# Feature-major outputs by stationary weight columns in a two-block float32 transformer kernel

## The chip, the cores and the metric

The kernel runs on one core of a Trainium2 chip. The metric is the device time of one execution in microseconds. A core has TensorE (matmuls, "PE" in the profile, and its weight loads, "PEld"), VectorE ("DVE"), ScalarE ("ACT"), GpSimd ("POOL") and SyncE ("SP", which issues most DMAs). A matmul multiplies a stationary operand (loaded first, 128 rows by up to 128 columns) with a moving one (128 rows by up to 512 columns) and adds into a bank of PSUM.

## The reference

For 256 tokens of width 2048, float32 throughout, the reference computes two transformer blocks in sequence:

```
x = x + concat(ssd(conv4(xbc)), fox_attention(q, k, v)) @ w_out      # z, xbc, dt, q, k, v, f = rmsnorm(x) @ w_in
x = x + peer(rmsnorm(x), wq, k1, k2, u, v)                           # expert search: q = t @ wq, scores q.k1, q.k2, top 16
x = rmsnorm(x)
h = x + concat(moba_attention(q, k, v), conformer_conv(u)) @ w_out2  # q, k, v, u = rmsnorm(x) @ w_in2, conv of 31 taps
h = h + cross_attention(rmsnorm(h), rmsnorm(mem), wq_c, wk_c, wv_c, wo_c)
h = h + square(relu(rmsnorm(h) @ w1)) @ w2
out = rmsnorm(h)
```

A convolution here runs along the tokens, one filter per channel. Attention scores contract over the features of q and k. So the convolutions, the attention scores and the expert scores all want the features of their input on partitions and the tokens along the free dimension.

## The kernel before

Every activation that feeds a GEMM lies in SBUF feature-major (features on partitions, 256 tokens along the free dimension) as two tiles: a rounded part (`xh`, type fp32r) and the remainder (`xl`). Weights stream from HBM as `raw` tiles of 512 rows x 512 columns. `split_w` cuts each into two halves of 256 rows; of each half ACT makes the rounded part `whi` (line 117) and DVE the remainder `wlo` (line 118). Both have three buffers. A product is the sum of three: high x high, high x low, low x high.

`gemm_block` (line 150 issues its matmuls) makes one block of 512 output columns from 2048 rows of weights: for each of 16 row groups and each of 2 halves of the tokens it loads 128 tokens of the activation as the stationary operand and moves 512 weight columns past them, three times. This is 96 matmuls of 512 columns. The result is token-major: tokens on partitions, 512 features along the free dimension. `gemm_cols` (lines 178 and 182) does it the other way for `peer_u` and `w1`: 128 weight columns are stationary, and the tokens move, 512 columns (high and low side by side) for the high weights, 256 for the low. Its result is feature-major.

Blocks whose result is wanted feature-major, but come from `gemm_block`, go through three steps. First ACT reads the accumulators and multiplies each token's row by its 1 / rms (`r`, one number per partition), into `pre`, `uv`, `scr` or `c_..`. Then TensorE transposes 128 x 128 pieces (`tpose`, line 226). Then ACT copies the result (`tposed`, line 604), or the convolution reads it from PSUM. The second convolution's evacuation (lines 1150 and 1151) applies the sigmoid gate before its transposes.

`by_token` (lines 197 to 205) turns `r` into rows, the same 256 numbers on every partition: DVE multiplies the identity by `r` into `dg`, one matmul with a matrix of ones adds the columns up, ACT copies the result to `rtok`. It is used by `up` and by the last feed-forward layer.

All work beside the GEMMs is written as generators. `later` puts one in a lane, and `step(rate)`, called four times a block, takes as many pieces from the lanes as the rates say; `flush` does the same, ahead of them, for what follows a block's evacuation. The framework then orders each engine's instructions by its own estimate of when they are ready; `pin` keeps one in place. Each engine runs its queue in order. PSUM holds two buffers each of the two accumulators, of `tp` (transposes) and of `mm` (small products).

Of the kernel before, what the change touches and what calls it, by code (L numbers as in the profile page):

```python
# [9 lines left out]
F32 = mybir.dt.float32  # L10
# [9 lines left out]
P = 128  # L20
# [35 lines left out]
def build(tc, A, out):  # L56
# [4 lines left out]
    with es:  # L61
# [127 lines left out]

        def sums(o, acc):  # L190
# [5 lines left out]
        def by_token(r, pool):  # L196

            dg = pool.tile([P, 2, P], F32, name="dg", bufs=1)
# [4 lines left out]
            o = pool.tile([P, T], F32, name="rtok", bufs=1)  # L203
            nc.scalar.copy(o, pr[:, :T])
            return o.unsqueeze(1).to_broadcast([P, 2, T])
# [84 lines left out]
def front(env):  # L290
# [5 lines left out]
    with phase_pool(tc, "ssd", True) as sp:  # L296
# [37 lines left out]
        z.gemm_block(xh, xl, range(16), src0, pre0.append, raw0=raw0)  # L334
# [6 lines left out]
        r8 = main.tile([P, 2], F32, name="rstd1q")  # L341
        nc.vector.tensor_scalar_mul(r8, r, 0.125)
# [94 lines left out]
        def conv(nb, sb):  # L437
            for c2 in range(0, 4, 2):
                tp = z.tpose(lambda j, t: sb[:, t, (c2 + j) * P : (c2 + j + 1) * P])
                for j in range(2):  # L440
                    ch = nb * 4 + c2 + j
                    w = V["conv_w"][:, ch * 4 : ch * 4 + 4]
                    o = cv[:, ch]
                    nc.vector.tensor_scalar(
                        o, tp[:, j], w[:, 3:4], V["conv_b"][:, ch : ch + 1], OP.mult, OP.add
                    )
                    for tap in range(3):
                        sh = 3 - tap
                        nc.vector.scalar_tensor_tensor(
                            o[:, sh:], tp[:, j, : T - sh], w[:, tap : tap + 1], o[:, sh:], OP.mult, OP.add  # L450
                        )
                    yield
                c = nb * 4 + c2
                nc.scalar.activation(cv[:, c : c + 2], cv[:, c : c + 2], AF.Silu)
# [13 lines left out]
        z.gemm_block(xh, xl, range(16), src(2), evac_xbc(2))  # L468
# [132 lines left out]
        def tposed(o, sb):  # L601
            for c2 in range(0, 4, 2):
                tp = z.tpose(lambda j, t: sb[:, t, (c2 + j) * P : (c2 + j + 1) * P])
                nc.scalar.copy(o[:, c2 : c2 + 2], tp)
                yield

        env["tposed"] = tposed

        def qkv(half, pool):
            sb = {}  # L610

            def evac(n):
                def f(acc):
                    if n == "v":
                        sb[n] = pool.tile([P, 2, 512], F32, name="v_f")
                    else:
                        sb[n] = fp.tile([P, 2, 512], F32, name="pre", bufs=2)
                    rr = r8 if n == "q" else r
                    pre = sb[n]
                    for t in range(2):  # L620
                        nc.scalar.activation(pre[:, t], acc[t], AF.Copy, scale=rr[:, t : t + 1])
                    yield
                    if n != "v":
                        sb[n] = pool.tile([P, 4, T], F32, name=n + "T")
                        yield from tposed(sb[n], pre)

                return f

            for i, n in enumerate("qkv"):
                z.gemm_block(xh, xl, range(16), src(5 + 3 * half + i), evac(n))  # L630
            return half, sb["q"], sb["k"], sb["v"]
# [122 lines left out]
def peer(env):  # L754
# [7 lines left out]
    with phase_pool(tc, "peer") as pp:  # L762
# [10 lines left out]
        def scores(nb):  # L773


            def f(acc):
                k12 = k12s[:, nb % 2]
                nc.sync.dma_start(k12, A["k12"][:, nb * 4 : nb * 4 + 4])
                sb = scr[:, 0].rearrange("p (t c) -> p t c", t=2)
                for t in range(2):  # L780
                    nc.scalar.activation(sb[:, t], acc[t], AF.Copy, scale=r2[:, t : t + 1])
                yield
                qT = scr[:, 1].rearrange("p (c t) -> p c t", c=4)
                yield from env["tposed"](qT, sb)
# [235 lines left out]

        for nb in range(4):
# [55 lines left out]
def second(env):  # L1077
# [6 lines left out]
    tposed = env["tposed"]  # L1084
    with phase_pool(tc, "mix2") as fp:
# [4 lines left out]

        ap = ExitStack()
# [21 lines left out]
        def norm_conv():  # L1113
# [30 lines left out]
        for c in range(0, 8, 2):  # L1144

            def ev(acc, c=c):
                uv = fp.tile([P, 2, 512], F32, name="uv", bufs=2)
                for t in range(2):
# [11 lines left out]
            z.gemm_block(nh, nl, range(16), src(c // 2), ev, RATES["conv"])  # L1160


        def qkv(half):
            sb = {}

            def evac(n):
                def f(acc):
                    if n == "v":
                        pre = sb[n] = att.tile([P, 2, 512], F32, name="v_m", bufs=2)
                    else:  # L1170
                        pre = fp.tile([P, 2, 512], F32, name="uv", bufs=2)
                    for t in range(2):
                        nc.scalar.activation(pre[:, t], acc[t], AF.Copy, scale=r[:, t : t + 1])
                    yield
                    if n != "v":
                        sb[n] = att.tile([P, 4, T], F32, name=n + "T", bufs=2)
                        yield from tposed(sb[n], pre)

                return f

            for h in range(half * 4, half * 4 + 4):
                nc.sync.dma_start(bias[:, h], toeplitz(z.bd[h]))
            for i, n in enumerate("qkv"):
                z.gemm_block(nh, nl, range(16), src(4 + 3 * half + i), evac(n), RATES["qkv%d" % half])
            return half, sb["q"], sb["k"], sb["v"]
# [50 lines left out]
        def ev(n, rs):  # L1236
            def f(acc):
                sb = fp.tile([P, 2, 512], F32, name="c_" + n, tag="uv", bufs=2)
                for t in range(2):
# [277 lines left out]
```

## Time and profile before

| | |
|---|---|
| median of 3 runs | 3170.79 us (3170.75 to 3173.59) |
| the profiled execution | 3171.58 us, its span 3169.8 us |
| granted TensorE clock, mean | 0.999 |
| TensorE matmuls busy | 3150.7 us (99%), 15732 matmuls |
| weight loads busy | 2604.8 us (82%), 15733 loads |
| DVE busy | 2080.7 us (66%) |
| ACT busy | 1603.6 us (51%) |

The span runs from the first to the last instruction; the rest of the execution's time lies around it. Busy time is the union of an engine's instructions. Matmuls overlap each other in it, so that TensorE's busy share says that it is never without work, not how fast it goes.

### The profile page before, as it was taken

What the parts mean: (1) busy time and instruction counts of PE and PEld (TensorE: products, weight loads), DVE (VectorE), ACT (ScalarE), POOL (GpSimd) and SP (SyncE); (2) the same over time, 40 slices, a digit from 0 to 9 for tenths busy, and PEclk for the clock granted to TensorE, in tenths of its full rate; (3) what the DMA queues carried; (4) which work ended last, traced back from release to release, by engine and by line L of the source; (5) the groups of instructions that cost most, each with busy time, mean ns of one, the idle gap of its engine ahead of it and who ended that gap; (6) DMA issues with size and microseconds to landing.
All of it is one profiled execution on the core that took longest, in us unless ns stands there. A gap on an engine that the chain in (4) does not pass through costs nothing.

```text
span 3169.8 us, 39966 instructions
## 1 busy us (share of the span) xinstructions
PE 3150.7 (99%) x15732; PEld 2604.8 (82%) x15733; DVE 2080.7 (66%) x3013; ACT 1603.6 (51%) x2191; POOL 91.2 (3%) x123
## 2 busy tenths in 40 slices
PE   8999999999999999999999999999999999999998
PEld 7877788888888888888788887888788888888887
DVE  5765667899777756565555555898666655555565
ACT  5556555665555545444444445445756534444454
POOL 0000000000000001001000000000000000000000
PEclk9999999999999999999999999999999999999999
DMA  6444454565677777677767665555444555555554
GB/s 251 173 146 165 144 188 175 207 213 206 233 242 246 246 255 264 235 239 265 265 227 238 233 217 180 194 186 184 161 174 172 186 186 189 191 191 186 187 190 155
DMA packets 101645, 648.52 MB, mean 205 GB/s; under 512 B 11229, under 2 KB 12389, under 8 KB 32592
## 3 DMA queue, kind: packets, MB, share of 16 engines
q1 hardware_dynamic: 82512, 575.63, 51.6%
q0 software_dynamic: 18944, 70.33, 6.7%
q8 instruction: 123, 2.02, 0.3%
q14 instruction: 66, 0.54, 0.0%
HBM read 608.68 MB, written 37.24 MB: 204 GB/s over the span
## 4 chain that ended last, share of the span: by engine, by line
PE 98%; DMA 1%; ACT 0%; DVE 0%; SPq 0%; issue 0%; ACTq 0%
PE acc L150 59%; PE acc L178 23%; PE acc L182 11%; PE tp L226 1%; PE mm L903 1%; PE mm L749 0%; DMA raw<-in_w_in_dram 0%; PE mm L641 0%; PE tp L740 0%; PE mm L788 0%; ACT whi L117 0%; PE mm L563 0%; PE mm L638 0%; PE mm L750 0%; DVE wlo L118 0%; DMA raw<-in_peer_v_dram 0%
## 5 line engine op out<-in xcount | busy, mean ns | idle before, releaser
L118 DVE TENSOR_TENSOR wlo<-raw,whi 128x1024 fp32r<-128x1024 f32 x1065 | 1301.2, 1223 | 937.4 <-ACT whi L117 935.2
L117 ACT CAST whi<-raw 128x1024 fp32r<-128x1024 f32 x1065 | 1115.4, 1048 | 1287.2 <-PE acc L150 886.2
L150 PE MATMUL acc<-whi,hT 128*128 128x512 f32 x5300 | 1700.4, 398 | 8.2 <-ACT whi L117 8.2
L150 PEld LDWEIGHTS acc<-whi,hT 128*128 128x128 f32 x5300 | 993.3, 188 | 249.1 <-ACT whi L117 8.7
L178 PE MATMUL acc<-hT,whi 128*128 128x512 f32 x3072 | 1086.1, 397 | 0.0
L150 PE MATMUL acc<-wlo,hT 128*128 128x512 f32 x2650 | 1048.6, 396 | 1.7 <-DVE wlo L118 1.6
L182 PE MATMUL acc<-hT,wlo 128*128 128x256 f32 x3072 | 863.4, 281 | 0.0
L178 PEld LDWEIGHTS acc<-hT,whi 128*128 128x128 f32 x3072 | 576.7, 188 | 136.2
L150 PEld LDWEIGHTS acc<-wlo,hT 128*128 128x128 f32 x2650 | 497.6, 188 | 120.1 <-DVE wlo L118 3.7
L182 PEld LDWEIGHTS acc<-hT,wlo 128*128 128x128 f32 x3072 | 578.9, 188 | 0.3 <-DVE wlo L118 0.2
L1107 DVE SCALAR_TENSOR_TENSOR cc<-hc,vec,cc 128x256 f32<-128x256 f32 x240 | 102.1, 478 | 0.5
L193 ACT COPY at<-acc 128x256 f32<-128x256 f32 x128 | 48.0, 375 | 81.9 <-PE acc L182 81.9
L194 DVE TENSOR_TENSOR at<-acc,at 128x256 f32<-128x256 f32 x128 | 53.5, 419 | 20.0 <-ACT at L193 19.5
L193 ACT COPY hid<-acc 128x256 f32<-128x256 f32 x64 | 23.9, 373 | 48.3 <-PE acc L182 48.3
L681 DVE TENSOR_TENSOR x<-acc,x 128x512 f32<-128x512 f32 x72 | 46.4, 681 | 0.7 <-PE acc L150 0.6
L923 DVE TENSOR_TENSOR at<-at,rtok 128x512 f32<-128x512 f32 x64 | 43.9, 686 | 1.1
L194 DVE TENSOR_TENSOR hid<-acc,hid 128x256 f32<-128x256 f32 x64 | 26.9, 421 | 21.0 <-ACT hid L193 21.0
L971 DVE TENSOR_TENSOR hT<-ag,hT 128x1024 fp32r<-128x1024 f32 x32 | 38.9, 1217 | 0.0
L967 DVE TENSOR_TENSOR ag<-ag 128x1024 f32<-128x1024 f32 x32 | 38.9, 1216 | 0.0
L927 POOL DMA_DIRECT2D act<-at x32 | 17.5, 547 | 730.7 <-ACT at L925 686.2
L952 POOL DMA_DIRECT2D ag<-gd x32 | 37.4, 1168 | 3.9 <-DMA gd<-gs 2.5
L903 PE MATMUL mm<-ohA,ohB 128*128 128x128 f16 x512 | 35.9, 220 | 0.0
(314 smaller groups left out, 1499.2 us busy)
## 6 DMA issues: line engine op xcount, KB each, us to landing
raw<-in_peer_u_dram SPq DMA_DIRECT2D x128, 1024.0 KB, 5.0
raw<-in_peer_v_dram SPq DMA_DIRECT2D x128, 1024.0 KB, 4.9
raw<-in_w_dram SPq DMA_DIRECT2D x128, 1024.0 KB, 4.9
raw<-in_w_in_dram SPq DMA_DIRECT2D x83, 1024.0 KB, 4.9
raw<-in_w_out_dram SPq DMA_DIRECT2D x32, 1024.0 KB, 4.8
raw<-in_wq_dram SPq DMA_DIRECT2D x16, 1024.0 KB, 4.9
act<-at POOLq DMA_DIRECT2D x32, 512.0 KB, 7.1
gd<-gs POOLq DMA_DIRECT2D x16, 1024.0 KB, 6.2
```

The costliest lines, as they stand in the source:

```text
L117: nc.scalar.copy(hi[:, :kt, :n], raw[:, k0 : k0 + kt, :n])
L118: nc.vector.tensor_sub(lo[:, :kt, :n], raw[:, k0 : k0 + kt, :n], hi[:, :kt, :n].bitcast(F32))
L150: mm(o, a, b, start=start, stop=stop)
L178: mm(acc[c], hi[:, k, cs], x2[:, kk].rearrange("p a t -> p (a t)"), start=kk == 0, stop=False,)
L182: mm(acc[c][:, :T], lo[:, k, cs], x2[:, kk, 0], start=False, stop=kk == 15)
L193: nc.scalar.copy(o[:, c], acc[c][:, T:])
L194: nc.vector.tensor_add(o[:, c], acc[c][:, :T], o[:, c])
L681: nc.vector.tensor_add(x[:, t, sl], acc[t], x[:, t, sl])
L903: mm(pg[:, j], B2[:, tq + j], Ag[k][:, tq + j], start=k == 0, stop=k == 1)
L923: nc.vector.tensor_mul(at[:, 2 * b : 2 * b + 2], at[:, 2 * b : 2 * b + 2], rt)
L967: z.pin(nc.vector.tensor_mul(av, av, g.rearrange("p b c t -> p c b t")))
L1107: nc.vector.scalar_tensor_tensor(o, hc[:, c, tap : tap + T], w[:, tap : tap + 1], o, OP.mult, OP.add)
```

## The change

A new function `gemm_feat` makes a block of 512 output columns with 128 weight columns stationary and 256 tokens moving: for each of 16 row groups and 4 groups of columns, three matmuls of 256 columns. Two column groups share an accumulator bank. It takes the place of `gemm_block` for the inputs of both convolutions, for q and k of the three attentions, and for the expert search's queries; v stays with `gemm_block`. `scaled` evacuates it on DVE: it multiplies each accumulator by the rows of 1 / rms (and by 0.125 for the first attention's q). The transposes, their copies and `tposed` go. `by_token` is called for the scale vectors of the first and the second convolution, of the memory and of the cross attention as well; that of the expert search moves ahead of its GEMMs. The gate of the second convolution becomes a sigmoid over the feature-major half and one multiply. The squares of the second convolution's layer norm are made one channel group at a time.

```
+        def gemm_feat(xh, xl, src, evac, rate=2, raw0=None):
+            acc = [ps.tile([P, 512], F32, name="acc%d" % c) for c in range(2)]
+            for g in range(4):
+                raw = raw0 if raw0 is not None and g == 0 else load_w(src(g))
+                for k0 in range(0, 4, 2):
+                    hi, lo = split_w(raw, k0)
+                    for k in range(2):
+                        kk = 4 * g + k0 + k
+                        for c in range(4):
+                            cs = slice(c * P, c * P + P)
+                            o = acc[c // 2][:, c % 2 * T : c % 2 * T + T]
+                            mm(o, hi[:, k, cs], xh[:, kk], start=kk == 0 and c % 2 == 0, stop=False)
+                            mm(o, hi[:, k, cs], xl[:, kk], start=False, stop=False)
+                            mm(o, lo[:, k, cs], xh[:, kk], start=False, stop=kk == 15 and c % 2 == 1)
+                    flush()
+                step(rate)
+            after = evac([a.rearrange("p (c t) -> p c t", c=2) for a in acc])
...
+        def scaled(o, acc, rows, by=None):
+            for c in range(2):
+                oc = o[:, 2 * c : 2 * c + 2]
+                if by is None:
+                    nc.vector.tensor_mul(oc, acc[c], rows)
+                else:
+                    nc.vector.scalar_tensor_tensor(oc, acc[c], by, rows, OP.mult, OP.mult)
...
-        z.gemm_block(xh, xl, range(16), src(1), pre0.append)
+        z.gemm_feat(xh, xl, src(1), pre0.append)
         z.drain()
         r = z.rstd_of(ss, D, "rstd1")
...
+        rt = z.by_token(r, fp)
...
         def conv(nb, sb):
-            for c2 in range(0, 4, 2):
-                tp = z.tpose(lambda j, t: sb[:, t, (c2 + j) * P : (c2 + j + 1) * P])
...
         def evac_xbc(nb):
             def f(acc):
-                sb = fp.tile([P, 2, 512], F32, name="pre", bufs=2)
-                for t in range(2):
-                    nc.scalar.activation(sb[:, t], acc[t], AF.Copy, scale=r[:, t : t + 1])
+                sb = fp.tile([P, 4, T], F32, name="pre", bufs=2)
+                z.scaled(sb, acc, rt)
                 z.later(conv(nb, sb))
...
+        z.later(rows_of_rstd())
         for nb in range(4):
-            z.gemm_block(th, tl, range(16), lambda g: A["wq"][nb, g], scores(nb), RATES["wq"])
-        rt = z.by_token(r2, pp)
-        z.pin(nc.tensor.ldweights(iota))
+            z.gemm_feat(th, tl, lambda g: A["wq"][nb, g], scores(nb), RATES["wq"])
+        rt = rts[0]
...
-                sq = fp.tile([P, 2, T], F32, name="sq", bufs=1)
-                nc.scalar.activation(sq, cc[:, c : c + 2], AF.Square)
                 for j in range(2):
-                    mm(pv[:, :T], C["ones"], sq[:, j], start=c + j == 0, stop=c + j == 7)
+                    sq = fp.tile([P, T], F32, name="sq", bufs=1)
+                    nc.scalar.activation(sq, cc[:, c + j], AF.Square)
+                    mm(pv[:, :T], C["ones"], sq, start=c + j == 0, stop=c + j == 7)
...
             def ev(acc, c=c):
-                uv = fp.tile([P, 2, 512], F32, name="uv", bufs=2)
-                for t in range(2):
-                    a, g = uv[:, t, :T], uv[:, t, T:]
-                    nc.scalar.activation(g, acc[t][:, T:], AF.Sigmoid, scale=r[:, t : t + 1])
-                    nc.vector.scalar_tensor_tensor(a, acc[t][:, :T], r[:, t : t + 1], g, OP.mult, OP.mult)
-                yield
-                tp = z.tpose(lambda j, t: uv[:, t, j * P : j * P + P])
-                nc.scalar.copy(hc[:, c : c + 2, 30:], tp)
+                uv = fp.tile([P, 4, T], F32, name="uv", bufs=2)
+                z.scaled(uv, acc, rows[0])
+                nc.scalar.activation(uv[:, 2:], uv[:, 2:], AF.Sigmoid)
+                yield
+                nc.vector.tensor_mul(hc[:, c : c + 2, 30:], uv[:, :2], uv[:, 2:])
                 z.later(conv(c))
...
-            z.gemm_block(nh, nl, range(16), src(c // 2), ev, RATES["conv"])
+            z.gemm_feat(nh, nl, src(c // 2), ev, RATES["conv"])
```

Where instructions stand now, at three places. First TensorE, at the second attention's q block. Before, the matmuls of the block after it are under way (each row is one matmul of the token-major form), and the four transposes of a part of q stand between them:

```order
L150 MATMUL acc_17237<-whi,hT 128x512
L150 MATMUL acc_17238<-whi,hT 128x512
L150 MATMUL acc_17238<-wlo,hT 128x512
L150 MATMUL acc_17238<-whi,hT 128x512
L226 MATMUL tp<-con,uv 128x128 x4
L150 MATMUL acc_17237<-whi,hT 128x512
L150 MATMUL acc_17237<-wlo,hT 128x512
L150 MATMUL acc_17237<-whi,hT 128x512
```

After, the same place on TensorE, where the q block (`acc_18359`) ends and the k block (`acc_18632`, `acc_18633`) begins; lines 202 to 204 are the three products of `gemm_feat`:

```order
L202 MATMUL acc_18359<-hT,whi 128x256
L203 MATMUL acc_18359<-hT,whi 128x256
L204 MATMUL acc_18359<-hT,wlo 128x256
L202 MATMUL acc_18632<-hT,whi 128x256
L203 MATMUL acc_18632<-hT,whi 128x256
L204 MATMUL acc_18632<-hT,wlo 128x256
L202 MATMUL acc_18632<-hT,whi 128x256
L203 MATMUL acc_18632<-hT,whi 128x256
L204 MATMUL acc_18632<-hT,wlo 128x256
L202 MATMUL acc_18633<-hT,whi 128x256
```

No transposes stand in the k block, and each matmul has half as many columns.

Second, DVE at the start of the second block (`mix2`), where the final scale `rstd` of the first is made, x is scaled by it in two halves (128x2048), and the first convolution block is evacuated. Before:

```order
L1065 TENSOR_TENSOR rstd_16349<-rstd_16349,rstd_16341 128x2
L1069 TENSOR_SCALAR x<-x,rstd_16341 128x2048
L118 TENSOR_TENSOR wlo<-raw,whi 128x1024 x5
L1151 SCALAR_TENSOR_TENSOR uv<-acc_16364,rstd_16349,uv 128x256
L1151 SCALAR_TENSOR_TENSOR uv<-acc_16365,rstd_16349,uv 128x256
```

After, at the same place:

```order
L1082 TENSOR_TENSOR rstd_17279<-rstd_17279,rstd_17271 128x2
L1086 TENSOR_SCALAR x<-x,rstd_17271 128x2048
L231 TENSOR_SCALAR dg<-con,rstd_17279 128x128 x2
L118 TENSOR_TENSOR wlo<-raw,whi 128x1024 x5
L217 TENSOR_TENSOR uv<-acc_17294,rtok 128x512
L217 TENSOR_TENSOR uv<-acc_17295,rtok 128x512
L118 TENSOR_TENSOR wlo<-raw,whi 128x1024
L1174 TENSOR_TENSOR hc<-uv 128x2x256
```

Two multiplies for `dg` come in ahead of the next `wlo`, the evacuation is twice as wide, and the gate's multiply follows it. On TensorE the `by_token` matmul stands behind 102 matmuls of the first convolution block and 8 transposes of x.

Third, DVE in the second convolution, around the evacuation of its second block; the `cc` rows are the taps. Before:

```order
L118 TENSOR_TENSOR wlo<-raw,whi 128x1024
L1107 SCALAR_TENSOR_TENSOR cc<-hc,vec,cc 128x256
L1151 SCALAR_TENSOR_TENSOR uv<-acc_16527,rstd_16349,uv 128x256
L1107 SCALAR_TENSOR_TENSOR cc<-hc,vec,cc 128x256
L1151 SCALAR_TENSOR_TENSOR uv<-acc_16528,rstd_16349,uv 128x256
L1107 SCALAR_TENSOR_TENSOR cc<-hc,vec,cc 128x256
L118 TENSOR_TENSOR wlo<-raw,whi 128x1024
```

After:

```order
L118 TENSOR_TENSOR wlo<-raw,whi 128x1024
L1130 SCALAR_TENSOR_TENSOR cc<-hc,vec,cc 128x256
L217 TENSOR_TENSOR uv<-acc_17559,rtok 128x512
L1130 SCALAR_TENSOR_TENSOR cc<-hc,vec,cc 128x256
L217 TENSOR_TENSOR uv<-acc_17560,rtok 128x512
L1130 SCALAR_TENSOR_TENSOR cc<-hc,vec,cc 128x256
L118 TENSOR_TENSOR wlo<-raw,whi 128x1024
L1130 SCALAR_TENSOR_TENSOR cc<-hc,vec,cc 128x256
L1174 TENSOR_TENSOR hc<-uv 128x2x256
```

The evacuation's two operations are wider, and a third follows. From the first tap to the last there are 248 convolution operations in both; 60 `wlo` rows stand among them before, 64 after.

## Rows read from the trace of the kernel before

**Rows 1.** The page: busy time by engine, and the chain that ended last

```profile
PE 3150.7 (99%) x15732; PEld 2604.8 (82%) x15733; DVE 2080.7 (66%) x3013; ACT 1603.6 (51%) x2191; POOL 91.2 (3%) x123
...
PE 98%; DMA 1%; ACT 0%; DVE 0%; SPq 0%; issue 0%; ACTq 0%
PE acc L150 59%; PE acc L178 23%; PE acc L182 11%; PE tp L226 1%; PE mm L903 1%; PE mm L749 0%; DMA raw<-in_w_in_dram 0%; PE mm L641 0%; PE tp L740 0%; PE mm L788 0%; ACT whi L117 0%; PE mm L563 0%; PE mm L638 0%; PE mm L750 0%; DVE wlo L118 0%; DMA raw<-in_peer_v_dram 0%
```

**Rows 2.** Busy time by stretch: length, PE, PEld, DVE, ACT, POOL, clock, DMA

```profile
2060.00:2160.00 100.00, 100.00 (x443) 80.65 (x442) 99.45 (x186) 45.09 (x51) 0.00 (x0) 1.00 0.52 184
...
2200.00:2250.00 50.00, 50.00 (x231) 40.82 (x230) 31.18 (x50) 28.69 (x49) 0.00 (x0) 1.00 0.61 207
```

**Rows 3.** Groups of transposes by operand: count, busy us, mean ns

```profile
L226 PE MATMUL tp<-con,pre 128*128 128x128 f32 x56 | 8.4, 273 | 0.0
...
L226 PE MATMUL tp<-con,uv 128*128 128x128 f32 x48 | 7.2, 272 | 0.0
...
L226 PE MATMUL tp<-con,scr 128*128 128x128 f32 x32 | 4.8, 272 | 0.0
...
L226 PE MATMUL tp<-con,c_q 128*128 128x128 f32 x8 | 1.3, 280 | 0.0
L226 PE MATMUL tp<-con,c_k 128*128 128x128 f32 x8 | 1.2, 272 | 0.0
```

**Rows 4.** The chain from 2113 to 2118 us: start us, us, what

```profile
2113.95 0.44 PE tp L226 x4
2114.39 2.80 PE acc L150 x12
```

**Rows 5.** PE in order of time, first and last of 48: start, us

```profile
56.14 0.28 PE L353 MATMUL mm<-hT,whi 128*32 128x256 f32 x1
...
61.62 0.28 PE L355 MATMUL mm<-hT,whi 128*32 128x256 f32 x1
```

**Rows 6.** The chain from 455 to 456.5 us, the expert scores

```profile
455.27 0.89 PE mm L788 x8
```

**Rows 7.** PE in order of time in two stages of `gemm_cols`

```profile
605.86 0.40 PE L178 MATMUL acc<-hT,whi 128*128 128x512 f32 x1
...
609.75 0.39 PE L178 MATMUL acc<-hT,whi 128*128 128x512 f32 x1
...
2695.70 0.39 PE L178 MATMUL acc<-hT,whi 128*128 128x512 f32 x1
...
2697.31 0.28 PE L182 MATMUL acc<-hT,wlo 128*128 128x256 f32 x1
2697.43 0.39 PE L178 MATMUL acc<-hT,whi 128*128 128x512 f32 x1
```

**Rows 8.** The chain from 517 to 518 us, where `by_token` runs

```profile
517.49 0.43 PE mm L202 x2
```

**Rows 9.** The chain from 2018 to 2026 us, convolution blocks 1 and 2

```profile
2022.63 0.44 PE tp L226 x4
```

**Rows 10.** DVE in order of time, from 2005 to 2011 us

```profile
2007.80 1.28 DVE L1069 TENSOR_SCALAR x<-x,rstd 128x2048 f32<-128x2048 f32 x1
```

**Rows 11.** Groups of DVE operations of 128 x 512: count, busy us, mean ns

```profile
L681 DVE TENSOR_TENSOR x<-acc,x 128x512 f32<-128x512 f32 x72 | 46.4, 681 | 0.7 <-PE acc L150 0.6
L923 DVE TENSOR_TENSOR at<-at,rtok 128x512 f32<-128x512 f32 x64 | 43.9, 686 | 1.1
```

**Rows 12.** DVE in order of time in the second convolution: start, us

```profile
2046.60 1.23 DVE L118 TENSOR_TENSOR wlo<-raw,whi 128x1024 fp32r<-128x1024 f32 x1
2047.74 2.06 DVE L1107 SCALAR_TENSOR_TENSOR cc<-hc,vec,cc 128x256 f32<-128x256 f32 x5
2049.82 1.22 DVE L118 TENSOR_TENSOR wlo<-raw,whi 128x1024 fp32r<-128x1024 f32 x1
```

**Rows 13.** PE in order of time at the layer norm's squares

```profile
2257.48 1.13 PE L1128 MATMUL mm<-sq,con 128*128 128x256 f32 x4 [0.23 <-ACT sq L1126]
```

**Rows 14.** Groups of weight loads: count, busy us, mean ns, idle before

```profile
L150 PEld LDWEIGHTS acc<-whi,hT 128*128 128x128 f32 x5300 | 993.3, 188 | 249.1 <-ACT whi L117 8.7 <-issue 3.9
...
L788 PEld LDWEIGHTS mm<-scr 128*128 128x128 f32 x64 | 8.2, 191 | 0.6
```

More of the change, by code (lines that the diff above doesn't have):

```diff
@@ L467, in front @@
         z.later(decays())
-        z.gemm_block(xh, xl, range(16), src(2), evac_xbc(2))
+        z.gemm_feat(xh, xl, src(2), evac_xbc(2))
         sz = sp.tile([P, 2, 1024], F32)
@@ L598, in front, with f @@
         z.later(ssd())
[L601 to L607, printed above, removed]
         def qkv(half, pool):
-            sb = {}
-            def evac(n):
-                def f(acc):
+            o = {n: pool.tile([P, 4, T], F32, name=n + "T") for n in "qk"}
+            o["v"] = pool.tile([P, 2, 512], F32, name="v_f")
+            for i, n in enumerate("qkv"):
+                def f(acc, n=n):
                     if n == "v":
-                        sb[n] = pool.tile([P, 2, 512], F32, name="v_f")
-                    else:
-                        sb[n] = fp.tile([P, 2, 512], F32, name="pre", bufs=2)
-                    rr = r8 if n == "q" else r
-                    pre = sb[n]
-                    for t in range(2):
[L621 to L631, printed above, removed]
+                        for t in range(2):
+                            nc.scalar.activation(o[n][:, t], acc[t], AF.Copy, scale=r[:, t : t + 1])
+                    else:
+                        z.scaled(o[n], acc, rt, 0.125 if n == "q" else None)
+                if n == "v":
+                    z.gemm_block(xh, xl, range(16), src(5 + 3 * half + i), f)
+                else:
+                    z.gemm_feat(xh, xl, src(5 + 3 * half + i), f)
+            return half, o["q"], o["k"], o["v"]
         def heads(half, qT, kT, v):
@@ L778, in f @@
                 nc.sync.dma_start(k12, A["k12"][:, nb * 4 : nb * 4 + 4])
-                sb = scr[:, 0].rearrange("p (t c) -> p t c", t=2)
-                for t in range(2):
-                    nc.scalar.activation(sb[:, t], acc[t], AF.Copy, scale=r2[:, t : t + 1])
+                qT = scr[:, 1].rearrange("p (c t) -> p c t", c=4)
+                z.scaled(qT, acc, rts[0])
                 yield
-                qT = scr[:, 1].rearrange("p (c t) -> p c t", c=4)
-                yield from env["tposed"](qT, sb)
                 for t in range(2):
@@ L1089, in src, with rows_of_rstd @@
             return lambda g: A["w_in2"][nb, g]
+        rows, rows_m = [], []
+        def rows_of_rstd():
+            rows.append(z.by_token(r, fp, ("mu", "rtok")))
+            yield
+        z.later(rows_of_rstd())
         ap = ExitStack()
@@ L1158, in ev @@
                 yield
-            z.gemm_block(nh, nl, range(16), src(c // 2), ev, RATES["conv"])
+            z.gemm_feat(nh, nl, src(c // 2), ev, RATES["conv"])
         def qkv(half):
[L1164 to L1179, printed above, removed]
+            o = {n: att.tile([P, 4, T], F32, name=n + "T", bufs=2) for n in "qk"}
+            o["v"] = att.tile([P, 2, 512], F32, name="v_m", bufs=2)
             for h in range(half * 4, half * 4 + 4):
@@ L1183, in qkv, with f @@
             for i, n in enumerate("qkv"):
-                z.gemm_block(nh, nl, range(16), src(4 + 3 * half + i), evac(n), RATES["qkv%d" % half])
-            return half, sb["q"], sb["k"], sb["v"]
+                def f(acc, n=n):
+                    if n == "v":
+                        for t in range(2):
+                            nc.scalar.activation(o[n][:, t], acc[t], AF.Copy, scale=r[:, t : t + 1])
+                    else:
+                        z.scaled(o[n], acc, rows[0])
+                if n == "v":
+                    z.gemm_block(nh, nl, range(16), src(4 + 3 * half + i), f, RATES["qkv%d" % half])
+                else:
+                    z.gemm_feat(nh, nl, src(4 + 3 * half + i), f, RATES["qkv%d" % half])
+            return half, o["q"], o["k"], o["v"]
         sc8 = 128 ** -0.5
@@ L1237, in f, with rows_of @@
             def f(acc):
[L1238 to L1241 removed]
                 if n == "v":
[L1243 to L1251 removed]
+                    sb = fp.tile([P, 2, 512], F32, name="c_v", tag="uv", bufs=2)
+                    for t in range(2):
+                        nc.scalar.activation(sb[:, t], acc[t], AF.Copy, scale=rs[:, t : t + 1])
+                else:
+                    sb = fp.tile([P, 4, T], F32, name="c_T" + n, tag={"q": "uv", "k": "ug"}[n], bufs={"q": 2, "k": 1}[n])
+                    z.scaled(sb, acc, rs[0])
+                ctile[n] = sb
+            return f
+        rows_5 = []
+        def rows_of(o, rs):
+            o.append(z.by_token(rs, fp, ("mu", "rtok")))
+            yield
+        rows_m.append(z.by_token(z.rm, fp, ("mu", "rv")))
+        z.gemm_feat(meh, mel, load_mem, ev("k", rows_m), RATES["mem_k"])
         while z.lanes[1]:
```

57 lines of the change are left out of this document (27 added, 30 removed).

## The prediction

> **What bounds the kernel now.** I read the page first: TensorE is busy for 99% of the span, and the chain that ended last is TensorE for 98% of it, nearly all of it matmuls of the three GEMM forms [rows 1]. So a change is worth what it adds to or takes from TensorE's own queue, unless another engine falls behind it. The table by stage says where that could happen: from 2060 to 2160 us DVE is busy for 99.45 of 100 us, in the one after it for far less (31.18 of 50 from 2200) [rows 2]. That stretch is the second convolution with the q, k, v blocks behind it; everywhere else DVE has room. The granted clock is full in all of these rows.
>
> **Transposes that go.** The groups by line show what is removed: transposes of `pre` (56), `uv` (48), `scr` (32), `c_q` (8) and `c_k` (8), together 152 [rows 3]. A group's mean (272 ns) overlaps its neighbours, so the price comes from the chain: four transposes hold TensorE for 0.44 us, and the matmuls around them keep their pace (12 in 2.80 us) [rows 4]. 152 x 0.11 = 16.7 us, all on the path. Their copies on ACT, and the scaled PSUM reads there, go too; ACT is busy for 51% and nothing on the chain waits for it, so I count that at nothing.
>
> **Matmuls that are cut in two.** 21 blocks change form: 3 of the first convolution, 4 q/k of the first attention, 4 of the expert search, 4 of the second convolution, 4 q/k of the second attention, q and k of the cross attention. Each has 96 matmuls of 512 columns now and gets 192 of 256: 2016 become 4032, each with a 128-column weight load. The columns stay the same, so the question is what a matmul costs beside its columns. Now: 2.80 / 12 = 233.3 ns apiece [rows 4]. 256 columns of the same type stand in the narrow `w_in_s` block: from the first to the last of its 48 are 47 steps in 61.62 - 56.14 = 5.48 us, 116.6 ns each, exactly half [rows 5]. There the weights are only 32 columns wide. Does a load of 128 fit under 256 columns? The score matmuls of the expert search load 128 f32 columns before each matmul; their load rows say 191 ns [rows 14], yet eight follow each other in 0.89 us, 111 ns apiece [rows 6]. So a new full load can be had every 111 ns, which is less than 116.6. The column-stationary blocks that exist (`gemm_cols`) show it in place: a matmul of 256 columns, during which the next full load runs, is followed after 0.12 us [rows 7]. I take 116.7, by the nearest row: 4032 x 116.7 - 2016 x 233.3 = +0.2 us. Bounds: five pairs of 512 + 256 in the second of rows 7 take 2695.70 to 2697.43, 0.346 a pair, or 115.3 per 256 columns, -5.6 us; eleven pairs of the first take 605.86 to 609.75, 0.3536, or 117.9, +4.6 us.
>
> The Trainium skill speaks against this cut: "TensorE: Matmul & The Clock Gate", section "Back-to-back issue gap", gives a matmul N / 2.4 + about 2.5 ns, so that 2016 more would cost an estimated 5.0 us, and "Perfetto Trace Analysis", section "Optimizing Tensor Performance", calls larger matmuls more efficient. The rows show another slope (233.3 for 512) and no fixed part; with the page's, the gain below would be 4.8 us smaller. The measurement decides.
>
> **What is added.** `by_token` now runs for four more scale vectors (the expert search's one only moves ahead). It is two passes of one f32 matmul, 0.43 us on the chain [rows 8]: +1.7 us. In three places it stands early in a block, behind a `dg` that DVE makes from a fresh rstd: in the second convolution DVE is done with the rstd and with scaling x at 2007.80 + 1.28 = 2009.1 [rows 10]. Block 1 there ends 12 matmuls before the transposes at 2022.63 [rows 9], at 2019.8, and with 96 matmuls and 8 transposes began at 2019.8 - 22.4 - 0.9 = 1996.5; 102 new matmuls and 8 transposes (12.8 us) later, at 2009.3, TensorE arrives. What is queued behind it on TensorE is the rest of that block. Nothing to 1 us at each of the three; I take +0.5 in all. In the first convolution the rstd is made while the second block still runs, and the small block of rows 5 (5.6 us) covers what follows. **Sum of this part +2.2 us.**
>
> Evacuation moves to DVE: two multiplies of 128 x 512 out of PSUM per block, 0.68 us by the like ones at lines 681 and 923 [rows 11], of which the next in DVE's queue waits for about 0.60, since rows there overlap by 0.09 (a split's row says 1.23, its step 1.14) [rows 12]. Of each block some splits stand ahead of it in DVE's order, and three `wlo` buffers of 2.8 us of matmuls each lie before TensorE would wait, so 1.2 us is covered, except where DVE is full. There I count. A split takes 2047.74 - 2046.60 = 1.14 us, five taps 2.06 less that overlap, 0.40 apiece. After the change 248 convolution operations stand between 64 splits (60 before), with three convolution evacuations of 3 x 0.60 and four of q and k of 2 x 0.60: 73.0 + 99.2 + 5.4 + 4.8 = 182.4 us, against 64 x 2.80 = 179.2 us on TensorE, attention left out on both. Before it was 60 x 1.14 + 99.2 + 2.4 (six reads of 0.4) = 170 against 168 and the transposes there. The lag of 3.2 us is about what the buffers hold: +1 us, between nothing and the whole added DVE work, 4 x 1.0 + 4 x 1.2 = 9 us.
>
> The squares of the second layer norm are now made one channel at a time through one buffer, eight round trips in place of four. TensorE already waits for one of them for 0.23 us [rows 13]; with 3 matmuls (0.70 us) between two trips and about as long a trip, +1 us, between nothing and 2.
>
> **The sum:** -16.7 + 0.2 + 2.2 + 1 + 1 = -12.3 us, -0.39%. The profiled execution took 3171.58 us (its span of 3169.8 and 1.8 around it), which gives 3159.3; it lay 0.8 above the median of the runs, 3170.79, so I forecast 3158.5 us.
>
> **Rivals.**
> 1. *Loads or weight changes show after all (slower).* The place is all 21 blocks. In the `up` stage two pairs of rows 7 take 2 x 0.3536 us against 2 x 0.346 in the last: 0.015 us more that returns with the matmul count and not with the columns. If it fell on every second 256-column matmul, it would be 2016 x 0.015 = +30 us: 3189 us. From 3 ns a matmul (119.7) the gain is gone, from 4.6 (121.3) the kernel is measurably slower. For it: no row shows a long run of 256-column matmuls with full fp32r loads. Against it: 111 ns a load [rows 6]. If it fell on every fourth, +15 us, 3174: no change that one can tell.
> 2. *Every load costs its row.* Loads last 188 ns at line 150 and 191 at 788 [rows 14]; if they could not overlap each other, a matmul would take 188: 4032 x 71 = +287 us, 3446 us. The 111 ns of rows 6 speak against it. The Trainium skill's "Perfetto Trace Analysis", section "Identifying the Most-Contended Engine", takes the weight loads' busy share as the measure of TensorE's headroom: by it 192 loads in a 22.4 us block would be over 100%. The trace has the eight loads of rows 6 at such a share.
> 3. *DVE becomes the bound in the second convolution.* All 9 us of its added work land on TensorE: about 3167 us, within 0.2%. For it: 99.45 of 100 [rows 2]. Against it: the taps are spread over four more splits, and DVE has room again from 2200.
> 4. *Weights standing still run faster,* as in the last of rows 7, and the waits don't show: -5.6 in place of +0.2, without the +2: 3151 us.
>
> **Numbers.** A measurement of this kernel can tell about 0.2% from no change, 6.3 us: faster is below 3164.4, slower above 3177.1. Likeliest (3154 to 3164): 0.66; rival 4: 0.11; rival 3: 0.09; rival 1: 0.12 (half of it slower, half within); rival 2: 0.02. Faster 0.77, same 0.15, slower 0.08. The range for 8 in 10 takes rivals 4 and 3 in: 3149 to 3170.
>
> **What the profile after would show.** Page: no transposes of `pre`, `uv`, `scr`, `c_q`, `c_k`; some 2000 matmuls and loads more; TensorE still on 98% of the chain. Chain: 192 matmuls of a feature block at 0.1167 us apiece, 22.4 us, the length of a block before. DVE: busy at 99% from 2040 to 2190, with TensorE's waits on `wlo` there at 0 to 3 us in all. What would make me wrong: a step of 0.120 or more in the feature blocks; waits on `wlo` of more than 5 us; a wait of several us at one `by_token`.

## The result and the profile after

The changed kernel takes 3132.03 us (median of 4 runs, 3131.77 to 3132.61) against 3170.82 us: a ratio of 0.9876, 95% interval 0.9859 to 0.9893. It is faster by 38.8 us where 12.3 were forecast, and lies below the range given (3149 to 3170). "Faster" was forecast, but for the most part it came by luck: the experiments below leave at most some 6 of the 38.8 us to the change itself.

The page of the changed kernel, the lines that answer to [rows 1]:

```profile
PE 3110.2 (99%) x17604; PEld 2699.0 (86%) x17604; DVE 2098.3 (67%) x3058; ACT 1571.3 (50%) x2130; POOL 91.3 (3%) x123
...
PE 99%; DMA 0%; ACT 0%; DVE 0%; SPq 0%; issue 0%; ACTq 0%
```

TensorE still sets the end, with 1872 more matmul records (2016 from the cut, 8 passes of `by_token`, less the 152 transposes of [rows 3], none of which is left), and it is still hardly ever without work. So the time must lie in how fast its matmuls follow each other. The table by stretch, in the second convolution and behind it, as [rows 2]:

```profile
2020.00:2120.00 100.00, 100.00 (x774) 97.29 (x773) 100.00 (x185) 38.01 (x37) 0.00 (x0) 1.00 0.56 199
2160.00:2210.00 50.00, 50.00 (x290) 43.99 (x289) 36.37 (x60) 25.89 (x42) 0.00 (x0) 1.00 0.50 178
```

DVE is full there, and TensorE is not without work for it. What TensorE waited for in the whole span (engine and line, whom for, us, times, longest):

```profile
PE acc L202 <- ACT whi L117: 7.4, 1, 7.4
PE acc L204 <- DVE wlo L118: 1.8, 2, 1.3
PE acc L150 <- ACT c_o L1340: 0.4, 1, 0.4
PE acc L150 <- DVE wlo L118: 0.3, 1, 0.3
```

The 7.4 us stand at the start of the kernel. Before the change it is much the same (its 8.2 us hold 7.5 at the start):

```profile
PE acc L150 <- ACT whi L117: 8.2, 2, 7.5
PE acc L150 <- DVE wlo L118: 1.6, 2, 1.0
PE acc L150 <- ACT c_o L1318: 0.4, 1, 0.4
PE mm L1128 <- ACT sq L1126: 0.2, 1, 0.2
```

No wait was added that matters, and none of 39 us was taken away. The new matmuls, second convolution, first and last of 334:

```profile
2019.73 0.28 PE L202 MATMUL acc<-hT,whi 128*128 128x256 f32 x1
...
2059.69 0.28 PE L202 MATMUL acc<-hT,whi 128*128 128x256 f32 x1
```

333 steps in 39.96 us: 120.0 ns each, where 116.7 were forecast. That is a loss. The gain is in a place that the diff does not touch, the experts' down stage, all `gemm_block` in both kernels. The chain over the same window, before and after (start, us, what):

```profile
1659.90 120.17 PE acc L150 x515
```

```profile
1659.88 120.13 PE acc L150 x530
```

120.17 / 515 = 233.3 ns, 120.13 / 530 = 226.7 ns, for the same instruction on the same shapes. With the time from each matmul's start to the next one's start summed over the two traces, up to a little above its usual pace and the rest put under gaps (us, count in brackets):

```
                          before           changed          difference
line 150                  1909.6 (8159)    1399.2 (6143)    2016 go: -471.8; the other 6143: -38.6
lines 202 to 204             -              485.6 (4032)    +485.6, or +13.8 with the 471.8
up and w1 (178, 182)      1081.7 (6144)    1079.6 (6144)    -2.1
transposes                  36.9 (410)       23.6 (258)     -13.3
other matmuls              105.8            106.3           +0.5
gaps and ends               35.7             34.5           -1.2
span                      3169.8           3128.8           -41.0
```

(471.8 is 2016 times 1909.6 / 8159. The transposes' row shows less than the 16.7 us forecast because the last transpose of a group is followed after 28 ns, and the matmul that follows takes a step of 316 in place of 233 ns; that part, some 3 us, stands under line 150 and gaps.) One line of this was not in the sum at all, and it is as large as the whole gain: 6143 untouched matmuls, 6.3 ns each.

What can move an untouched matmul? The diff also takes out a tile of 8 bytes a partition, `rstd1q`, in the pool that lies below the weight stream. `raw`, `whi` and `wlo` therefore begin 32 bytes lower: the first `whi` at 113792 in place of 113824, while `hT` stays at 22144. Below, the *distance* is (weight tile - hT) modulo 512: 32 before, 0 after, the same for all six `whi` and `wlo` buffers, which are 4096 bytes apart.

### The profile page after: what moved, and what is told of

It is laid out like the page before. It is cut to its first block, busy times and chain, and to the rows that moved or that the text cites. A ratio compares the mean times of both kernels' runs of the same rounds, so it can differ in the third digit from the quotient of the medians.

```text
span 3128.8 us, 43755 instructions
## 1 busy us (share of the span) xinstructions
PE 3110.2 (99%) x17604; PEld 2699.0 (86%) x17604; DVE 2098.3 (67%) x3058; ACT 1571.3 (50%) x2130; POOL 91.3 (3%) x123
## 4 chain that ended last, share of the span: by engine, by line
PE 99%; DMA 0%; ACT 0%; DVE 0%; SPq 0%; issue 0%; ACTq 0%
PE acc L150 44%; PE acc L178 23%; PE acc L182 12%; PE acc L202 5%; PE acc L204 5%; PE acc L203 5%; PE mm L914 1%; PE tp L257 1%; PE mm L763 0%; PE mm L655 0%; DMA raw<-in_w_in_dram 0%; PE tp L754 0%; PE mm L799 0%; PE mm L591 0%; PE mm L652 0%; PE mm L764 0%
## 5 line engine op out<-in xcount | busy, mean ns | idle before, releaser
L150 PE MATMUL acc<-whi,hT 128*128 128x512 f32 x4020 | 1256.1, 391 | 0.0
L150 PEld LDWEIGHTS acc<-whi,hT 128*128 128x128 f32 x4020 | 754.0, 188 | 158.6 <-issue 3.1
L182 PE MATMUL acc<-hT,wlo 128*128 128x256 f32 x3072 | 859.4, 280 | 0.0
L150 PE MATMUL acc<-wlo,hT 128*128 128x512 f32 x2010 | 783.3, 390 | 0.3 <-DVE wlo L118 0.3
L178 PEld LDWEIGHTS acc<-hT,whi 128*128 128x128 f32 x3072 | 576.8, 188 | 137.0
L182 PEld LDWEIGHTS acc<-hT,wlo 128*128 128x128 f32 x3072 | 579.6, 189 | 0.1
L150 PEld LDWEIGHTS acc<-wlo,hT 128*128 128x128 f32 x2010 | 377.5, 188 | 78.1 <-DVE wlo L118 0.7
L202 PE MATMUL acc<-hT,whi 128*128 128x256 f32 x1280 | 367.0, 287 | 7.4 <-ACT whi L117 7.4
L204 PE MATMUL acc<-hT,wlo 128*128 128x256 f32 x1280 | 362.9, 284 | 1.8 <-DVE wlo L118 1.8
L203 PE MATMUL acc<-hT,whi 128*128 128x256 f32 x1280 | 362.9, 284 | 0.0
L202 PEld LDWEIGHTS acc<-hT,whi 128*128 128x128 f32 x1280 | 246.0, 192 | 9.9 <-ACT whi L117 7.7
L204 PEld LDWEIGHTS acc<-hT,wlo 128*128 128x128 f32 x1280 | 245.6, 192 | 2.5 <-DVE wlo L118 2.5
L203 PEld LDWEIGHTS acc<-hT,whi 128*128 128x128 f32 x1280 | 246.2, 192 | 0.4
L225 DVE TENSOR_TENSOR at<-acc,at 128x256 f32<-128x256 f32 x128 | 53.3, 418 | 15.5 <-ACT at L224 14.4
L224 ACT COPY hid<-acc 128x256 f32<-128x256 f32 x64 | 23.9, 374 | 49.0 <-PE acc L182 49.0
```

The costliest lines, as they stand in the source:

```text
L150: mm(o, a, b, start=start, stop=stop)
L178: mm(acc[c], hi[:, k, cs], x2[:, kk].rearrange("p a t -> p (a t)"), start=kk == 0, stop=False,)
L182: mm(acc[c][:, :T], lo[:, k, cs], x2[:, kk, 0], start=False, stop=kk == 15)
L202: mm(o, hi[:, k, cs], xh[:, kk], start=kk == 0 and c % 2 == 0, stop=False)
L203: mm(o, hi[:, k, cs], xl[:, kk], start=False, stop=False)
L204: mm(o, lo[:, k, cs], xh[:, kk], start=False, stop=kk == 15 and c % 2 == 1)
```

## Experiments

My theory: the distance sets the pace. The rival: something else in the change does (the transposes gone, the pinned weight load gone, the other order of work).

**e1, the kernel before without the slot.** The order of the work is that of before; distance 0.

```
-        r8 = main.tile([P, 2], F32, name="rstd1q")
+        r8 = fp.tile([P, 2], F32, name="rstd1q", bufs=1)
```

> The kernel before, with its 8-byte tile rstd1q taken from another pool, so that raw, whi and wlo begin 32 bytes lower (whi at 113792 in place of 113824, a multiple of 64) and nothing else changes; the order of the work is that of before. Theory (the place of the weight tiles sets the pace of the unchanged matmuls): a 512-column step at line 150 falls from 233.3 to 226.8 ns; 7950 of them make -52 us, so about 3119 us, which is less than the changed kernel. Rival (the pace comes from something else that the change does, such as the removed transposes, the removed pinned weight load or the shorter queue): the step stays at 233.3 and the time at 3171 us.

3123.81 us (ratio 0.9849, 0.9833 to 0.9866). The chain in the down stage:

```profile
1659.90 120.14 PE acc L150 x530
```

226.7 ns. Moving one 8-byte tile gains 47.2 us, more than the change did, and the pinned weight load and all transposes are still there. The rival falls.

**e2, the changed kernel with the slot.** Distance 32.

```
+        r8 = main.tile([P, 2], F32, name="rstd1q")
+        nc.vector.tensor_scalar_mul(r8, r, 0.125)
         rt = z.by_token(r, fp)
```

> The changed kernel with the 8-byte tile rstd1q put back (written, not read), so that raw, whi and wlo lie where they lay before (whi at 113824). Theory of the place: line 150 goes back to 233.3 ns (6030 x 6.5 = +39 us), and the 256-column steps of lines 202 to 204 to the 116.7 of the narrow block before (4032 x -3.2 = -13 us): about 3158 us, the time that was forecast. If only the first holds, 3171 us. Rival (the pace comes from something else in the change): 226.8 and 119.9 ns stay, 3132 us.

3164.65 us (ratio to before 0.998, 0.9971 to 0.999). The chain in the down stage, then the new matmuls, first and last of 340:

```profile
1659.93 120.17 PE acc L150 x515
```

```profile
2019.77 0.28 PE L202 MATMUL acc<-hT,whi 128*128 128x256 f32 x1
...
2059.89 0.28 PE L202 MATMUL acc<-hT,whi 128*128 128x256 f32 x1
```

Line 150 is back at 233.3 ns; the new form is at 40.12 / 339 = 118.3 ns, not at 116.7. So with the tiles where they lay, **the change itself gains 6.3 us** (3 to 9 by the interval of the ratio); the other 32.6 us (3164.65 to 3132.03) are the place. And with both at distance 0 the change loses: e1 is 8.2 us below the changed kernel.

**e3 and e4, the operands moved apart and together.** e3: `hT` 32 bytes higher, weights 128 higher (distance 96). e4: all 32 higher (distance 0).

```
+        pad = const.tile([P, 8], F32)                      # both
         epsc = const.tile([P, 1], F32)
+        r8 = main.tile([P, 24], F32, name="rstd1q")        # e3 alone
```

> The changed kernel with hT 32 bytes higher (22176, no multiple of 64) and the weight tiles still at a multiple of 64 (113920). In line 150 the stationary operand is now the one off the multiple, in lines 202 to 204 and the column-stationary blocks of up and w1 the moving one. If the place of the moving operand alone decides, line 150 stays at 226.8 and the 256-column steps grow by some 3 ns (+13 us, 3145 us) if they grow as the 512-column ones did. If the place of the two operands to each other decides, line 150 is at about 233.3 and lines 202 to 204 at about 116.7 or another value than 119.9: 3158 us. If hT's place does not matter, 3132 us.

> The changed kernel with hT and the weight tiles both 32 bytes higher (22176 and 113824). If the place of the two to each other decides, it is as the changed kernel: 226.8 and 119.9 ns, 3132 us. If the weight tiles' own place decides, as with rstd1q put back: line 150 at 233.3, about 3158 to 3171 us. Rival (place does not matter): 3132 us as well, which e1 and e2 tell apart from the first.

e3: 3150.23 us (0.9933, 0.9917 to 0.995). e4: 3131.10 us (0.9874, 0.9858 to 0.989). The chains in the down stage, e3 and then e4:

```profile
1659.89 120.17 PE acc L150 x515
```

```profile
1659.85 120.36 PE acc L150 x531
```

e4 is the changed kernel again (226.7) although every address differs from it by 32: the distance counts, not the place to a multiple of 64. e3 has 233.3 although its weights lie at a multiple of 64. It is 14.4 us faster than e2 by its pairs of 512 + 256 in up and w1, which are at 346.7 ns throughout. Lines 202 to 204 add less than 1 us: 117.3 ns in the second convolution, but 118.0 over all blocks against 118.1 in e2.

**s1, s2 and s3, the distance scanned.** The tiles get spare columns and each block uses a view that begins some bytes in; `raw` stays. In s1 and s2 the slots are 4224 bytes apart (128 modulo 512), in s3 4608, which is 0 modulo 512. The lines of s3:

```
-            hi = wp.tile([P, 2, 512], F32R, name="whi", bufs=3)
+            hi = wp.tile([P, 1024 + 128], F32R, name="whi", bufs=3)
...
+            hi, lo = (a[:, off : off + 1024].rearrange("p (a n) -> p a n", n=512) for a in (hi, lo))
```

> The changed kernel with whi and wlo tiles 128 bytes longer, in which each block places both parts a number of bytes behind the tile's beginning (a multiple of 128, as hT's): 0, 4, 8, 16, 24, 32, 40, 48, 56, 60, 64, 96 in turn, counted apart for the three forms of block; raw stays where it is. Only the steps of the trace count, not the time. If the distance of the two operands modulo 64 sets the pace: line 150 at 227 ns for 0 and 64, 233 for 32 and 96; lines 202 to 204 at 119.8 and 118.0; the offsets between tell whether the pace follows the distance gradually or jumps. If raw's place did it in the first four runs (raw moved with whi there), all offsets have the pace of the changed kernel.

> The same with hT and the beginning of the weight tiles 32 bytes higher. If only the distance counts, every offset has the pace that it has in the other scan; if the place to a line of 64 bytes counts as well, the blocks of up and w1 change: with hT 32 off and the weights at a multiple of 64 (offsets 32 and 96 here) 229.3 and 117.4 ns, as with hT alone moved, and something else at offset 0.

> The changed kernel with whi and wlo slots of 4608 bytes (raw with two buffers in place of three to make room), so that all six slots are at the same distance from hT modulo 512 and only the offset of a block's view changes it: 0, 32, 64, 96, 128, 160, 192, 256, 320, 384, 448, 480 in turn. Only steps of the trace count. If the distance modulo 64 decides: 227 ns for line 150's steps at multiples of 64 and 233 else; 119.8 and 118.0 for the 256-column steps of the new form. If the distance modulo 512 decides (the first scans had slots 128 bytes apart and found 231 at 0): only offset 0 gives 227 and the others differ, 114 ns for the new form at 64 or at another offset.

One run each (3156.17, 3155.97 and 3194.22 us; the third waits for its two `raw` buffers). Mean step in ns by distance in s3, gaps left out (pair: a 512 and a 256 step of up and w1):

```
distance          0     32     64     96    128    192    256    320    448    480
line 150        227.0  233.3  229.0  233.4  233.2  233.3  227.5  229.2  233.3  233.3
lines 202-204   119.9  118.3  115.6  117.9  118.7  117.3  119.8  117.8  117.8  116.7
pair            350.2  353.1  352.9  346.7  351.0  349.6  352.2  353.0  350.0  346.9
```

The scan had 160 and 384 as well: about 234.2, 119.9 and 350.2 ns, and 232.5, 119.8 and 350.6. Modulo 64 is not enough: 64 and 192 are other paces than 0. Whether 512 is the period was not shown: in line 150 the pace at 256 is close to that at 0, and at 320 to that at 64. In s1 and s2, whose slots are 128 bytes apart modulo 512, offset 0 gave no flat 226.7 either. The chain there in a block of offset 0, s1 and then s2:

```profile
1534.93 18.26 PE acc L159 x79
```

```profile
1534.93 18.25 PE acc L159 x79
```

231.1 and 231.0 ns, between the paces of the distances that the six slots have there: all six must lie right. With every address 32 bytes on, the pace is the same again. `raw`, which moved with `whi` in the first four runs, stood still in the scans, so it is not what counts.

**e5, the weights 64 higher.** Distance 64 in the whole kernel.

```
+        r8 = main.tile([P, 16], F32, name="rstd1q")
```

> The changed kernel with the weight tiles 64 bytes higher, all six slots (whi at 113856; distance to hT 64 modulo 512). If the distance modulo 64 decides: 3132 us as the changed kernel. If modulo 512: the 256-column steps at 114.3 ns as in the first scans at offset 64 (4032 x -5.5 = -22 us) and line 150 between 226.8 and 231 (0 to +25 us): 3110 to 3135 us.

3137.24 us (0.989, 0.9874 to 0.9907), just above the span that was expected. The chain in the down stage, and lines 202 to 204, first and last of 358:

```profile
1659.78 120.40 PE acc L150 x526
```

```profile
1999.41 0.28 PE L202 MATMUL acc<-hT,whi 128*128 128x256 f32 x1
...
2039.87 0.28 PE L202 MATMUL acc<-hT,whi 128*128 128x256 f32 x1
```

228.9 ns, and 40.46 / 357 = 113.3 ns: in these blocks the new form takes half of the best 512-column pace. It does not everywhere: by block it is 113.3 to 117.8 ns in this run, 114.8 over all. What it gains, some 19 us, line 150 and the pairs of up and w1 (353.3) give back.

**e6, the transposes made twice.** The forecast's largest term by itself.

```
+                    for _ in range(times):        # 2 for pre, uv, scr, c_q, c_k
                         nc.tensor.transpose(tp[:, c, t * P : t * P + P], src(c, t), ident)
```

> The kernel before with each of the 152 transposes that the change removes made twice, into the same place (1 copy more each, nothing else; the placement stays). The prediction's price, 0.11 us each on TensorE's path: +16.7 us, 3187.7 us. Rival (part of it was hidden, so that removing them gains less): under +10 us. Rival (a transpose changes the pace of what follows and costs more): over +20 us.

3187.58 us against 3170.32 (1.0053, 1.0039 to 1.0067): +17.3 us for 152. In its chain eight hold TensorE where four did in [rows 4], and the 12 matmuls between take 2.81 us, as before:

```profile
2125.20 0.87 PE tp L227 x8
2126.07 2.81 PE acc L150 x12
```

**e7 and e8, each kernel with each form well placed.** `hT` tiles get 512 spare bytes, and each activation begins where its main use wants it. e7 is e1 with distance 480 for up and w1; e8 is the changed kernel with distance 64 for the inputs of both blocks and the memory, 480 for the expert search with up and for w1.

```
-            x2 = main.tile([P, KD, 2, T], F32R, name="hT", tag="hT", bufs=2)
+            x2 = main.tile([P, KD * 2 * T + 128], F32R, name="hT", tag="hT", bufs=2)
+            x2 = x2[:, off // 4 : off // 4 + KD * 2 * T].rearrange("p (k a t) -> p k a t", k=KD, a=2)
...
-    th, tl, th2 = z.new_hT()
+    th, tl, th2 = z.new_hT(32)
```

> The kernel before with rstd1q out of the way as in e1, and hT views that begin 32 bytes later where its columns move (up with the expert search, w1), in tiles 512 bytes longer; the second attention's softmax has two buffers in place of three to make room. Steps from the scans: up pairs 350.3 to 346.9 (2048 x -3.4 = -7 us), w1 pairs 353 to 347 (1024 x -6 = -6 us), the expert search's 384 matmuls 227 to 233 (+2.4 us). From 3123.8: about 3113 us. If the pace is a matter of chance in each build, it stays near 3124 or goes up.

> The changed kernel with the same hT tiles: views 448 bytes in (weights 64 beyond, modulo 512) for the inputs of both blocks and the memory, 32 bytes in for the expert search with up, and for w1, none elsewhere. Steps from the scans: 3072 feature matmuls 119.8 to 114.6 (-16 us), 768 to 116.7 (-2.4 us), about 900 of line 150 in the same stages 227 to 229 (+1.8 us), up and w1 pairs to 346.9 (-7 and -5 us). From 3132.0: about 3103 us, 10 us under the kernel before placed likewise; so the change itself would gain about 10 us when each form lies best, where it lost 8 at distance 0 and gained 6 at 32. If the pace is a matter of chance in each build, it stays near 3132 or goes up.

e7: 3112.97 us (0.982, 0.9807 to 0.9834). e8: 3107.59 us (0.98, 0.9787 to 0.9814), the fastest here, 63 us below the kernel before. e7 in `up`, first and last of 671 (670 pairs), and e8 in the second convolution, first and last of 346:

```profile
523.94 0.40 PE L178 MATMUL acc<-hT,whi 128*128 128x512 f32 x1
...
756.22 0.39 PE L178 MATMUL acc<-hT,whi 128*128 128x512 f32 x1
```

```profile
1990.10 0.28 PE L203 MATMUL acc<-hT,whi 128*128 128x256 f32 x1
...
2029.22 0.28 PE L203 MATMUL acc<-hT,whi 128*128 128x256 f32 x1
```

232.28 / 670 = 346.7 ns a pair, 39.12 / 345 = 113.4 ns. The paces of the scan carry over. e7 came out within 0.1 us of its expectation, e8 4.6 us above: the sums of its steps are within 1 us of what was expected, but the gaps between matmuls grew by 5.6 us against the changed kernel (18.3 to 23.9 in the sum of starts). Between the two, the change is worth 5.4 us, under the 0.2% that I said a measurement can tell, though no run of the one lies in the span of the other. So what the edit is worth hangs on the place: 6.3 us gained at distance 32, 8.2 lost at 0, 5.4 gained here.

**e9, the load's read alone moved.** No tile moves; the down stage's weight loads begin some tokens into `hT`, the same ones for both halves.

```
-                            tsl = slice(t * P, t * P + P)
+                            tsl = slice(t * P, t * P + P) if at is None else slice(at, at + P)
```

> The changed kernel, in which the eight experts' down blocks (32 blocks of line 150, no tile moved) load as the stationary operand the 128 tokens that begin 0, 8, 16, 64, 112, 96, 48 and 1 tokens into hT, for both halves, so that it leaves out the right order of tokens in them. The read of the weight load moves by 0, 32, 64, 256, 448, 384, 192 and 4 bytes, everything that is written or moved stays. If it is the load's read beside the read of the moving operand that sets the pace, the steps follow the scan at the same distances: 227, 233, 233, 227.5, 229, 233, 229, over 233 ns, about +10 us in all. If the place of a tile sets it in another way (who writes it, where its slot begins), all stay at 227 and the time at 3132 us.

One run, 3143.40 us. The chain, one window in each expert, shifted by 0, 32, 64, 256, 448, 384, 192 and 4 bytes:

```profile
1309.85 15.19 PE acc L150 x67
...
1354.85 55.30 PE acc L150 x237
...
1444.91 37.35 PE acc L150 x160
...
1534.85 55.31 PE acc L150 x244
...
1621.93 56.08 PE acc L150 x245
...
1711.98 53.22 PE acc L150 x229
...
1799.99 55.16 PE acc L150 x241
...
1889.81 19.06 PE acc L150 x82
```

226.7, 233.3, 233.4, 226.7, 228.9, 232.4, 228.9 and 232.4 ns. A shift by s makes the distance -s; the scan has 227.0, 233.3, 233.3, 227.5, 229.0, 233.2 and 229.2 there for the first seven, within 0.8 ns. Tiles, writers and slots are the same in all eight, and in e4 both operands moved and the pace stayed, so **where the weight load reads, against where the moving operand is read, sets the pace of line 150.** How the memory behind it is cut up no run here shows.

## Why the prediction was wrong

**The step that failed** stands in its first part: "a change is worth what it adds to or takes from TensorE's own queue". The sum held the pace of every untouched matmul at 233.3 ns [rows 4], as if it belonged to the instruction. In line 150 it goes with the placing of two operands, which the diff moved: e1, e2 and e9 show 226.7 and 233.3 for the same instruction, and 38.6 us of the difference lie there. A row that could have warned me was shown: the pairs of [rows 7], the same instructions at 353.6 in one stage and 346 in another, from which I made bounds and rival 1, and did not ask why they differ. (Both lie at distance 32, so the place is not what parts these two; see the last section.)

- **Transposes, -16.7:** right. 17.3 us for doubling them (e6), which is 0.114 us each.
- **The cut of matmuls, +0.2 (-5.6 to +4.6):** mis-sized. At the old place 4032 steps take 479.0 us by their starts against 471.8, +7.2; in the changed kernel +13.8. The 116.6 of [rows 5] was of a block whose loads hold 32 columns and step on by 128 bytes, so that its distance runs through 32, 160, 288 and 416; it did not carry to 118.3 with 128 columns. Those 7 us account for the difference between -12.3 and the -6.3 of e2. The bounds took a third of a 512 + 256 pair for the new step, which [rows 7] do not show; by their own numbers they come to about -5.4 and +4.9.
- **Rival 1 (loads show):** its size came, 120.0 ns at distance 0, and its sign did not, since the place of the weights gave more elsewhere. As a mechanism it falls: with as many loads the step is 113.3 in e5, so there is no fixed price for a load that returns. Rival 4 (weights standing still run faster) did not come: 118.3 and 120.0 are slower than 116.7.
- **by_token, +2.2:** right within some tenths. Five of the six calls hold TensorE for 0.43 us on the chain after too, the one in the second convolution for 0.59, and no wait at them is among the waits above.
- **DVE, +1, and the layer norm's squares, +1:** both smaller. Waits on `wlo` are 2.1 us in all where they were 1.6, while DVE is full from 2020 to 2120. The eight pairs of squares take 0.43 to 0.55 us each on the chain, some 0.4 in all beyond 0.43. Rival 3 did not come.
- **The Trainium skill:** "TensorE: Matmul & The Clock Gate", section "Wait — 56ns, not 53.3ns?", gives a warm matmul N / 2.4 + about 2.5 ns, an estimated 215.8 ns for 512 columns. No trace here has it: 226.7 is the lowest long run. The same page's "Back-to-back issue gap", which the prediction drew on, gives that formula for an isolated matmul and other spacings for a stream of loads and matmuls, which the prediction left out. "SBUF — State Buffer", section "SBUF: two separate sides", says that "PE, ACT, and DVE's dedicated pair never wait on anyone". That is said of engines that wait for each other; it does not speak of TensorE's own two reads, whose places alone make 226.7 to 233.4 in e9.

## What to carry to other kernels

Before a change is costed or credited, compare the pace of the instructions that it does not touch in both traces; and compare addresses in the two builds, since one small tile more or less moves all that lies behind it. An A/B in which the placement moved measures the placement too: put the old slot back, as in e2, to see what the edit itself is worth. Where long runs of matmuls set the time, a scan over view offsets, several in one kernel, can pay: here it led to 1.8% in the kernel before (e7) and to 0.8% in the changed one (e8), with the same work, and each form of matmul wanted its own distance.

## What the runs showed of the hardware

**Several paces lie 16 cycles of the full clock apart.** At 2.4 GHz (granted clock 1.00 in these stretches) 226.7 and 233.3 ns are 544 and 560 cycles for 512 columns, 113.3 and 120.0 are 272 and 288 for 256, and the pairs 346.7 and 353.3 are 832 and 848 for 768: beyond the columns 32 or 48 cycles, 16 or 32, and 64 or 80. Others lie between, such as 228.9 (549 cycles), 232.4, 118.3 and 117.3 ns; in the 228.9 of e5 the single steps take turns from 225 to 232 ns.

**One distance can hold two paces.** In the changed kernel at distance 0, `up` from behind the eight score matmuls at 518.37 us and then `w1`, first and last row of each:

```profile
519.61 0.40 PE L178 MATMUL acc<-hT,whi 128*128 128x512 f32 x1
...
751.87 0.40 PE L178 MATMUL acc<-hT,whi 128*128 128x512 f32 x1
...
2587.70 0.39 PE L178 MATMUL acc<-hT,whi 128*128 128x512 f32 x1
...
2677.79 0.40 PE L178 MATMUL acc<-hT,whi 128*128 128x512 f32 x1
```

670 pairs in 232.26 us, 346.7 each; 255 pairs in 90.09 us, 353.3 each. The same code at the same distance keeps one pace for hundreds of matmuls and another later. Nearly every change of pace in this trace falls where other matmuls or a gap come between two runs of pairs: in front of the eight score matmuls the pairs of `up` took 353 ns. What picks the one or the other was not tried; at distances 96 (e3) and 480 (e7, e8) the long runs of pairs had 346.7 alone.
